# Fixed tiles for split transposes and probabilities, residual rows on DVE, other banks at the end of the FFN, and GpSimd low parts in two pieces, in a two-layer trunk on one core

## The chip, the core and the metric

One Trainium2 chip, of which the kernel uses one core. The metric is the device time of one execution in microseconds (us). Engines are named as the profile names them: PE (matrix multiplications), PEld (its weight loads), DVE (vector), ACT (scalar), POOL (GpSimd) and SP (which only issues DMAs here). Each engine works through its own list of instructions strictly in order; an instruction whose input is not ready holds up all that stand behind it on that engine.

## The reference

Two post-norm decoder layers on x of 1 x 1024 tokens x 1024 channels in float32. Layer 0 mixes with a causal pooling mixer and a Mamba-2 scan, layer 1 with two kinds of attention of eight heads each; after each mixer comes a SwiGLU network (FFN), and both have a residual and a LayerNorm.

```python
def block_causal_attention(q, k, v, log_decay_cum):      # 8 heads, 64 wide
    sc = jnp.einsum('bhqd,bhkd->bhqk', qi, k).astype(F32) * scale
    if fi is not None:                                    # FoX: forgetting gate
        sc = sc + fi[..., :, None] - log_decay_cum[:, :, None, :]
    sc = jnp.where(kpos[None, :] <= qpos[:, None], sc, -jnp.inf)
    p = jax.nn.softmax(sc, axis=-1).astype(v.dtype)
    return jnp.einsum('bhqk,bhkd->bhqd', p, v)

def odd_mixer(x, ...):                                    # layer 1
    o_fox = block_causal_attention(heads(qf), heads(kf), heads(vf), fcum)
    o_mla = block_causal_attention(q, k, kv[..., MLA_NOPE:], None)   # low-rank q and kv
    return jnp.concatenate([o_fox, o_mla], axis=-1) @ w_out

def swiglu(x, w_gate, w_up, w_down):
    return (jax.nn.silu(x @ w_gate) * (x @ w_up)) @ w_down

for l in range(2):
    h = even_mixer(x, ...) if l % 2 == 0 else odd_mixer(x, ...)
    x = layer_norm(DEEPNORM_ALPHA * x + h, ln_mix_g[l], ln_mix_b[l])
    x = layer_norm(DEEPNORM_ALPHA * x + swiglu(x, ...), ln_ffn_g[l], ln_ffn_b[l])
```

## The kernel before

**Split operands.** Every float32 operand of a product is split in two: `hi` (L196, ACT) rounds it to the matmul's own type, and `lo` (L204, or L206 with a scale; DVE, or GpSimd where the caller says so) subtracts that from the original. A product is then three matmuls: high by high, low by high, high by low (L237 to L239 for projections, L499 to L501 in the FFN, L635 to L637 in its second half, L1600 for scores, L1670 for probabilities by values, where one tile holds both parts). Weights are loaded raw (`load_raw`, L225, tile `wr`), then split into `wh` and `wl`.

**Slots.** Nearly all tiles of 128 x 1024 come from one pool, `big`, of 50 slots (`self.slot`). The tile library decides when the kernel is built, by a scheduler that walks the program in its written order and starts what is ready, in which order each engine's instructions stand and which slot a tile gets. A tile in a slot that another tile held must wait until every instruction that used the old tile has ended; that wait stands in the instruction that writes the new tile.

**Attention** (about 1090 to 1930 us of the execution). Sixteen heads come in eight pairs, four of FoX and then four of MLA. `chain` walks them in steps (head, block of 256 queries); `filler` lets the projections of the coming pairs, with their weight loads (`units_y`), run in between. A step is: scores on PE (`qk`, L1600), row maximum on DVE (L1621 or L1625), exponential on ACT (L1623 or L1626), scaling on DVE (L1631), all in a tile `prob`; then `pv` turns the probabilities by PE transposes (L1652) into a PSUM bank `p`, splits each into a tile `pt` (high part on ACT by L196, low part on DVE by L204; the triangular block goes to a tile `diag` that is kept for it), multiplies with the values (L1670) and adds the two halves of the result (`otmp` on ACT L1674, `ot` on DVE L1675). Both `prob` and `pt` take a slot of the pool for each use. PE does all this in order, so a `pt` that is late holds it.

**Residual rows.** While the attention runs, a generator `late` rescales the residual of the first layer for the second: eight times it loads 128 rows (SP queue, tile `resr`), multiplies and adds on GpSimd (L442, L443) and stores the rows by a DMA on GpSimd's queue (L444). `chain` advances it at every odd step from the second pair on (L1747).

**FFN.** Each block of the hidden layer takes seven products; each goes to a PSUM bank that `bank()` hands out from the cycle `turn` of six tags (L504): `p0` to `p3` are four banks and `pa` two more. DVE adds the products up (L527 to L542). `second()` then starts its own products (L635) in `p0` to `p3`. There are 146 calls of `bank()` in each FFN; 146 is 24 times 6 and 2 more, so the last two products (i = 4 and i = 3, added up in L542 and L540) lie in the first two banks of the cycle.

**Weight loads ahead.** `units_y` keeps `ahead + dma_ahead` raw weights loading ahead of their use (L837), `dma_ahead` being 2.

## Time and profile before

| | |
|---|---|
| time, median of 3 runs | 2545.56 us (2543.9 to 2548.15) |
| profiled execution | 2546.77 us |
| its span (first to last instruction) | 2544.7 us |
| mean granted TensorE clock | 0.986 of full speed |
| PE busy | 2449.8 us (96%) |
| DVE busy | 1824.6 us (72%) |
| ACT busy | 1044.6 us (41%) |
| POOL busy | 758.2 us (30%) |

The profiled execution lies 1.2 us above the median, and 2.07 us of it lie outside the span. PE is at work nearly all the time, so the span is what PE must do plus what it stands still, 94.9 us in all. "Busy" includes that a matmul takes longer where the clock is low: of the two levels, full speed is 2.4 GHz (1.0) and the lower is 1.2 GHz (0.5); the mean over a stretch tells how the two were mixed. In a list of waits, "A <- B" says that A stood still until B had ended.

### The profile page before, as it was taken

The numbers are of one execution on the slowest core, as the hardware profiler recorded it, in microseconds if no ns is written. First come the engines' busy times: TensorE is split into PE (matmuls) and PEld (weight loads), VectorE is DVE, ScalarE is ACT, GpSimd is POOL, SyncE is SP. The second block draws the span as 40 slices with busy tenths as digits, with TensorE's granted clock in tenths as the row PEclk, the third lists the DMA queues.
The fourth block names the chain that finished last, engine by engine and source line by source line (L and its number), as shares of the span: only waits on it lengthen the run. The fifth ranks groups of instructions, "written<-read, shape, count | busy, mean of one in ns | idle before, by whom it ended". The sixth has DMA issues, their size and how long they took to land. (4 is left out here: it accounts for less than half of the span.)

```text
span 2544.7 us, 31623 instructions
## 1 busy us (share of the span) xinstructions
PE 2449.8 (96%) x11886; PEld 2002.8 (79%) x11886; DVE 1824.6 (72%) x2907; ACT 1044.6 (41%) x1758; POOL 758.2 (30%) x446
## 2 busy tenths in 40 slices
PE   8999999999999999999998899998999999999998
PEld 6788877778888878887786777777877888887887
DVE  4365554788777779974645467787779778777988
ACT  3343344352222234454544356665544232233453
POOL 2454442113443441111113333111011433433113
PEclk9999999999999999999999899998999999999999
DMA  4111114124333347332011122012322433426641
GB/s 172 50 34 42 34 42 164 56 79 153 133 133 128 133 168 283 119 105 96 26 50 62 63 69 63 19 42 93 115 83 95 149 121 124 149 99 257 215 153 71
DMA packets 95257, 269.87 MB, mean 106 GB/s; under 512 B 9952, under 2 KB 10208, under 8 KB 95104
## 3 DMA queue, kind: packets, MB, share of 16 engines
q1 hardware_dynamic: 85632, 234.75, 26.8%
q0 software_dynamic: 6720, 23.13, 2.5%
q10 hardware_dynamic: 2752, 9.96, 1.1%
q8 instruction: 94, 1.54, 0.3%
q14 instruction: 59, 0.48, 0.1%
HBM read 190.08 MB, written 75.50 MB: 104 GB/s over the span
## 5 line engine op out<-in xcount | busy, mean ns | idle before, releaser
L204 DVE TENSOR_TENSOR w<-wr,w 128x512 fp32r<-128x512 f32 x440 | 415.7, 968 | 105.4 <-ACT w L196 99.6
L196 ACT CAST w<-wr 128x512 fp32r<-128x512 f32 x440 | 251.6, 619 | 424.2 <-DVE wr L482 331.7
L499 PE MATMUL p<-x,w 128*128 128x512 f32 x848 | 331.9, 393 | 6.4 <-ACT w L196 4.8
L500 PE MATMUL p<-x,w 128*128 128x512 f32 x848 | 331.2, 391 | 0.1
L501 PE MATMUL p<-x,w 128*128 128x512 f32 x848 | 331.2, 391 | 0.0
L547 POOL TENSOR_TENSOR h<-h,c 128x1024 f32<-128x1024 f32 x44 | 114.5, 2602 | 572.3 <-DVE c L540 420.2
L204 POOL TENSOR_TENSOR wl<-wr,wh 128x1024 fp32r<-128x1024 f32 (+2 forms) x55 | 128.2, 2333 | 358.7 <-ACT wh L196 292.0
L499 PEld LDWEIGHTS p<-x,w 128*128 128x128 f32 x848 | 159.7, 188 | 43.2 <-ACT w L196 6.3
L500 PEld LDWEIGHTS p<-x,w 128*128 128x128 f32 x848 | 159.8, 188 | 33.6 <-DVE x L204 1.2
L501 PEld LDWEIGHTS p<-x,w 128*128 128x128 f32 x848 | 159.7, 188 | 33.7 <-DVE w L204 0.8
L499 PE MATMUL pa<-x,w 128*128 128x512 f32 x384 | 149.4, 389 | 0.0
L500 PE MATMUL pa<-x,w 128*128 128x512 f32 x384 | 149.4, 389 | 0.0
L501 PE MATMUL pa<-x,w 128*128 128x512 f32 x384 | 149.4, 389 | 0.0
L239 PE MATMUL pa<-xh,wl 128*128 128x512 f32 x368 | 144.4, 392 | 4.4 <-POOL wl L204 4.4
L237 PE MATMUL pa<-xh,wh 128*128 128x512 f32 x368 | 146.7, 399 | 1.9 <-ACT u L904 1.1
L238 PE MATMUL pa<-xl,wh 128*128 128x512 f32 x368 | 144.1, 392 | 0.0
L635 PE MATMUL p<-w,h 128*128 128x512 f32 x352 | 136.9, 390 | 3.6 <-DVE c L542 3.6
L636 PE MATMUL p<-w,h 128*128 128x512 f32 x352 | 137.4, 391 | 1.9 <-DVE w L204 1.8
L637 PE MATMUL p<-w,h 128*128 128x512 f32 x352 | 136.8, 389 | 0.0
L204 DVE TENSOR_TENSOR h<-hr,h 128x512 fp32r<-128x512 f32 x154 | 123.4, 801 | 10.8 <-ACT h L196 10.7
L196 ACT CAST h<-hr 128x512 fp32r<-128x512 f32 x154 | 95.3, 619 | 73.9 <-DMA hr<-parts 37.6
L1652 PE MATMUL p<-con,prob 128*128 128x128 f32 x576 | 95.4, 283 | 8.6 <-DVE pt L204 4.9
(408 smaller groups left out, 6024.8 us busy)
## 6 DMA issues: line engine op xcount, KB each, us to landing
hr<-parts SPq DMA_DIRECT2D x70, 512.0 KB, 4.2
wr<-in_ffn_w_gate_dram SPq DMA_DIRECT2D x44, 512.0 KB, 3.8
wr<-in_ffn_w_up_dram SPq DMA_DIRECT2D x44, 512.0 KB, 4.2
wr<-in_ffn_w_down_dram SPq DMA_DIRECT2D x44, 512.0 KB, 8.8
parts<-s SPq DMA_DIRECT2D x80, 256.0 KB, 2.1
accr<-rows SPq DMA_DIRECT2D x32, 512.0 KB, 3.6
parts<-h SPq DMA_DIRECT2D x60, 256.0 KB, 2.1
wr<-in_even_wt_dram SPq DMA_DIRECT2D x24, 512.0 KB, 3.8
```

The source lines that it names most:

```text
L196: self.nc.scalar.copy(out=out, in_=in_)
L204: eng.tensor_tensor(out=out, in0=in_, in1=hi.bitcast(F32), op=ALU.subtract)
L237: mm(out=out, lhsT=lh, rhs=rh, start=i == 0, stop=False)
L238: mm(out=out, lhsT=lh, rhs=rl, start=False, stop=False)
L239: mm(out=out, lhsT=ll, rhs=rh, start=False, stop=i == n - 1)
L499: mm(out=out, lhsT=ah, rhs=b[k][:, lo], start=k == 0, stop=False)
L500: mm(out=out, lhsT=ah, rhs=b[k][:, hi], start=False, stop=False)
L501: mm(out=out, lhsT=al, rhs=b[k][:, lo], start=False, stop=k == 3)
L547: pt(out=h, in0=h, in1=c, op=ALU.mult)
L635: mm(out=out, lhsT=ah, rhs=b[:, lo], start=first, stop=False)
L636: mm(out=out, lhsT=ah, rhs=b[:, hi], start=False, stop=False)
L637: mm(out=out, lhsT=al, rhs=b[:, lo], start=False, stop=last)
```

## The change

Six edits. `lo` on GpSimd splits a tile of more than 512 columns into two operations (512 and the rest). The two operations of `late` on the residual rows go to DVE; a pause is put between them, and `chain` advances `late` at every step instead of every odd one, so that a row still takes two steps; the load stays on SP's queue, the store on GpSimd's. The cycle of FFN banks begins with `pa`, `pa`. `dma_ahead` is 1 in the odd layer. `pt` has two fixed tiles and `prob` four, which are taken from the pool once and handed out in turn.

```diff
--- before.py
+++ after.py
@@ -200,7 +200,10 @@
 
     def lo(self, out, in_, hi, scale=None, eng=None):
         eng = eng or self.nc.vector
-        if scale is None:
+        if eng is self.nc.gpsimd and scale is None and len(out.shape) == 2 and out.shape[1] > 512:
+            for s in (slice(0, 512), slice(512, out.shape[1])):
+                eng.tensor_tensor(out=out[:, s], in0=in_[:, s], in1=hi[:, s].bitcast(F32), op=ALU.subtract)
+        elif scale is None:
             eng.tensor_tensor(out=out, in0=in_, in1=hi.bitcast(F32), op=ALU.subtract)
         else:
             eng.scalar_tensor_tensor(out=out, in0=in_, scalar=scale, in1=hi.bitcast(F32),
@@ -439,8 +442,9 @@
             yield
             for t in range(NT):
                 r = self.load_raw(store[t * P:(t + 1) * P, :], name="res")
-                nc.gpsimd.tensor_tensor(out=r, in0=r, in1=v[0], op=ALU.mult)
-                nc.gpsimd.tensor_tensor(out=r, in0=r, in1=v[1], op=ALU.add)
+                nc.vector.tensor_tensor(out=r, in0=r, in1=v[0], op=ALU.mult)
+                yield
+                nc.vector.tensor_tensor(out=r, in0=r, in1=v[1], op=ALU.add)
                 nc.gpsimd.dma_start(out=store[t * P:(t + 1) * P, :], in_=r)
                 yield
 
@@ -501,7 +505,7 @@
                 mm(out=out, lhsT=al, rhs=b[k][:, lo], start=False, stop=k == 3)
 
         hid = {}
-        turn = itertools.cycle(("p0", "p1", "p2", "p3", "pa", "pa"))
+        turn = itertools.cycle(("pa", "pa", "p0", "p1", "p2", "p3"))
 
         def bank():
             tag = next(turn)
@@ -1573,6 +1577,7 @@
 
         def filler():
             self.grain = self.odd_grain
+            self.dma_ahead = 1
             misc_weight()
             self.preload(units, self.pre_n, ws)
             for g, u in zip(lead, units):
@@ -1609,10 +1614,10 @@
             prob = []
             n = [x.shape[1] for x in S]
             if sum(n) <= 1024:
-                t = self.slot(name="prob")
+                t = turn("prob")
                 prs = [t[:, :n[0]], t[:, n[0]:n[0] + n[1]]]
             else:
-                prs = [self.slot(name="prob")[:, :x] for x in n]
+                prs = [turn("prob")[:, :x] for x in n]
             l = self.small((P, 2), "l", bufs=6)
             for i, (s, pr) in enumerate(zip(S, prs)):
                 nk = n[i]
@@ -1637,6 +1642,13 @@
             for c in (0, 512):
                 nc.vector.tensor_copy(out=t[:, c:c + P], in_=self.zerob)
 
+        kept = {n: [self.slot(dt=d, name=n) for _ in range(c)] for n, d, c in (("pt", F32R, 2), ("prob", F32, 4))}
+
+        def turn(n):
+            if not kept[n]:
+                return self.slot(dt=F32R if n == "pt" else F32, name=n)
+            return kept[n][self.turn_of(n, len(kept[n]))]
+
         def pv(prob, vv, u, ot, e):
             nj = 2 * u + 2
             hl = {}
@@ -1651,7 +1663,7 @@
                         if j <= 2 * u + x:
                             nc.tensor.transpose(out=ps[:, c:c + P], in_=prob[x][:, j * P:(j + 1) * P],
                                                 identity=self.ident)
-                t = diag[self.turn_of("diag", self.n_diag)] if last else self.slot(dt=F32R, name="pt")
+                t = diag[self.turn_of("diag", self.n_diag)] if last else turn("pt")
                 b = P if last else 0
                 self.hi(t[:, b:512], ps[:, b:512])
                 self.lo(t[:, 512 + b:1024], ps[:, b:512], t[:, b:512])
@@ -1744,7 +1756,7 @@
                     products, nF, vv = pr[0][e]
                     if pend and self.tr_first[kind]:
                         next(pend[0])
-                    if n and i % 2:
+                    if n:
                         next(late, None)
                     prob, scale = softmax(qk(products, u), nF)
                     pend.append(pv(prob, vv, u, pr[1], e))
```

Counted in the kernel before, the lines from L204 on stand three lower after the change, from L443 on four, from L1576 on five and from L1645 on twelve.

How the order of instructions moves shows at three places. In these rows a name ends in a number that tells tiles apart; `PE`, `DVE`, `Activation` and `Pool` in the brackets are engines that the instruction waits for, `DMAHW` a DMA of SP's or ACT's queue, `DMASW` one of GpSimd's.

ACT at about 1345 to 1365 us of the execution, in the FoX pairs, before: exponentials (L1623), high parts of the transposes (L196 `pt`, `diag`), squares of the latent rows (L1395), and one weight.

```order
L1623 ACTIVATE prob_10440,l_10442<-prob_10440,nm_10443 128x640 [waits DVE_49]
L1623 ACTIVATE prob_10441,l_10442<-prob_10441,nm_10446 128x768 [waits DVE_49,Activation_49]
L196 CAST pt_10455<-p_1617_10450 128x512 [waits DMASW1_49,PE_49,Pool_49]
L196 CAST diag_8972<-p_1620_10473 128x384 [waits PE_49,Activation_49]
L1395 ACTIVATE sq_10365<-p_1603_10366 128x512 [waits DVE_49,PE_49,Activation_49]
L1674 COPY otmp_10493<-p_1616_10449 64x256 [waits PE_49]
L1623 ACTIVATE prob_10511,l_10513<-prob_10511,nm_10514 128x640 [waits DVE_49]
L1623 ACTIVATE prob_10512,l_10513<-prob_10512,nm_10517 128x768 [waits DVE_49]
L1395 ACTIVATE sq_10365<-p_1619_10460 128x512 [waits DVE_49]
L196 CAST pt_10532<-p_1630_10527 128x512 [waits PE_49,Pool_49]
L196 CAST wh_10540<-wr_10163 128x1024 [waits DMAHW0_49,PE_49]
L196 CAST pt_10558<-p_1638_10553 128x512 [waits Pool_49]
```

The same stretch on ACT after (L1628 is the exponential, L1686 the copy to `otmp`):

```order
L1628 ACTIVATE prob_9007,l_10455<-prob_9007,nm_10456 128x640 [waits DVE_49]
L196 CAST pt_9006<-p_1590_10463 128x512 [waits PE_49,Activation_49]
L1628 ACTIVATE prob_9008,l_10455<-prob_9008,nm_10459 128x768 [waits DVE_49]
L196 CAST diag_9002<-p_1592_10485 128x384 [waits PE_49,Activation_49]
L1686 COPY otmp_10505<-p_1589_10462 64x256 [waits PE_49,Activation_49]
L1628 ACTIVATE prob_9009,l_10525<-prob_9009,nm_10526 128x640 [waits DVE_49]
L196 CAST wh_10377<-wr_10180 128x1024 [waits DMAHW7_49,PE_49]
L1628 ACTIVATE prob_9010,l_10525<-prob_9010,nm_10529 128x768 [waits DVE_49]
L196 CAST pt_9005<-p_1600_10539 128x512 [waits PE_49]
L196 CAST pt_9006<-p_1607_10565 128x512 [waits PE_49,Activation_49]
L1628 ACTIVATE prob_9007,l_10624<-prob_9007,nm_10625 128x384 [waits DVE_49]
L196 CAST diag_9002<-p_1608_10588 128x384 [waits PE_49,Activation_49]
```

All three `pt` before wait for GpSimd, and the first also for a DMA of its queue; after, the `pt` wait for PE and for ACT's own earlier work, and they stand in the two tiles 9005 and 9006 in turn. `prob` stands in the tiles 9007 to 9010 in turn. Over the whole attention 18 of the 96 casts to `pt` wait for GpSimd before and none after.

DVE at the first residual rows, before (no row of `late` is on DVE; L1621 is the row maximum, ISA a custom operation, L1629 the reciprocal, L1631 the scaling):

```order
L204 TENSOR_TENSOR diag_8972<-p_1573_10222,diag_8972 128x384 [waits Activation_49]
L1621 ISA prob_10262,nm_10267<-pa_10255,nF_10192 128x1024 [waits PE_49]
L1621 ISA nm_10267 128x1
L1675 TENSOR_TENSOR ot_9410<-p_1572_10221,otmp_10238 64x256 [waits Activation_49]
L1394 COPY craw_10169<-p_1558_10171 128x512 [waits PE_49]
L1629 RECIPROCAL l_10263<-l_10263 128x2 [waits Activation_49]
L1631 TENSOR_SCALAR prob_10261<-prob_10261,l_10263 128x896 [waits DVE_49]
L1631 TENSOR_SCALAR prob_10262<-prob_10262,l_10263 128x1024
L204 TENSOR_TENSOR diag_8972<-p_1585_10277,diag_8972 128x384 [waits Activation_49]
L1675 TENSOR_TENSOR ot_10199<-p_1584_10276,otmp_10296 64x256 [waits Activation_49]
```

And after, with L445 and L447 the multiplication and addition of the residual rows:

```order
L207 TENSOR_TENSOR diag_9002<-p_1555_10243,diag_9002 128x384 [waits Activation_49]
L1626 ISA prob_9009,nm_10285<-pa_10275,nF_10210 128x1024 [waits PE_49]
L1626 ISA nm_10285 128x1
L1687 TENSOR_TENSOR ot_9448<-p_1554_10242,otmp_10259 64x256 [waits Activation_49]
L445 TENSOR_TENSOR resr_10266<-resr_10266,lnv_10218 128x1024 [waits DMAHW4_49,DMAHW0_49,DMAHW6_49,DMASW7_49,Pool_49]
L1634 RECIPROCAL l_10281<-l_10281 128x2 [waits Activation_49]
L447 TENSOR_TENSOR resr_10266<-resr_10266,lnv_10220 128x1024 [waits DMASW0_49,DVE_49]
L1636 TENSOR_SCALAR prob_9008<-prob_9008,l_10281 128x896 [waits DVE_49]
L207 TENSOR_TENSOR diag_9002<-p_1564_10295,diag_9002 128x384 [waits Activation_49]
L1636 TENSOR_SCALAR prob_9009<-prob_9009,l_10281 128x1024
```

The two operations of a row of 128 stand among the softmax and the low parts; L445 waits for the load (`DMAHW`), and behind it stand the reciprocal and the scaling of the step.

ACT where the last MLA weights go over to the output projection, before: loads from `spill` that ACT itself issues (L225; others come by SP) and the casts to `wh`.

```order
L196 CAST qh_13705<-qr_13704 128x1024 [waits DVE_49,Pool_49]
L196 CAST diag_8972<-p_2328_13931 128x384 [waits PE_49]
L196 CAST wh_13886<-wr_13330 128x1024 [waits DMAHW6_49]
L225 DMA wr_13890<-spill 128x1024
L196 CAST wh_13892<-wr_13698 128x1024 [waits DMAHW7_49]
L1674 COPY otmp_13945<-p_2302_13853 64x256 [waits PE_49]
L196 CAST wh_13898<-wr_13884 128x1024 [waits DMAHW1_49]
L225 DMA wr_13902<-spill 128x1024
L196 CAST wh_13904<-wr_13890 128x1024 [waits DMAHW2_49]
L196 CAST wh_13910<-wr_13896 128x1024 [waits DMAHW3_49]
L196 CAST wh_13914<-wr_13902 128x1024 [waits DMAHW4_49]
L196 CAST wh_13918<-wr_13908 128x1024 [waits DMAHW5_49]
```

And after (L228 is the load, L1631 the exponential):

```order
L196 CAST qh_13623<-qr_13622 128x1024 [waits DVE_49]
L228 DMA wr_13795<-spill 128x1024
L196 CAST wh_13797<-wr_13615 128x1024 [waits DMAHW6_49,Pool_49]
L1686 COPY otmp_13861<-p_2156_13765 64x256 [waits PE_49]
L1631 ACTIVATE prob_9009,l_13876<-pa_13867,nm_13877 128x128 [waits DVE_49]
L196 CAST pt_9006<-p_2188_13884 128x512 [waits PE_49]
L196 CAST wh_13803<-wr_13795 128x1024 [waits DMAHW0_49]
L196 CAST pt_9005<-p_2189_13897 128x512 [waits PE_49]
L228 DMA wr_13808<-spill 128x1024
L196 CAST wh_13810<-wr_13801 128x1024 [waits DMAHW1_49]
L1631 ACTIVATE prob_9009,l_13876<-pa_13867,nm_13880 128x256 [waits DVE_49]
L196 CAST pt_9006<-p_2191_13916 128x512 [waits DVE_49,PE_49]
```

Before, seven casts `wh` stand nearly together, and the tile `wr_13698` that the second of them reads was loaded 26 rows earlier; after, ACT's first load, `wr_13795`, stands five rows ahead of its cast, and casts of `pt` and exponentials stand between the casts to `wh`.

## Rows read from the trace of the kernel before

**Rows 1.** The page, busy time by engine: us, share of the span, instructions.

```profile
PE 2449.8 (96%) x11886; PEld 2002.8 (79%) x11886; DVE 1824.6 (72%) x2907; ACT 1044.6 (41%) x1758; POOL 758.2 (30%) x446
```

**Rows 2.** Windows: length, busy us of PE, PEld, DVE, ACT, POOL, clock, DMA share, GB/s.

```profile
1088.00:1920.00 832.00, 774.06 (x4187) 629.14 (x4186) 558.35 (x1095) 428.80 (x819) 172.76 (x102) 0.97 0.20 65
1344.00:1408.00 64.00, 57.04 (x269) 43.09 (x269) 35.68 (x67) 29.95 (x60) 22.36 (x11) 0.92 0.21 66
1408.00:1472.00 64.00, 57.02 (x292) 46.70 (x291) 34.21 (x66) 26.55 (x50) 18.86 (x11) 0.89 0.18 58
1472.00:1536.00 64.00, 56.39 (x283) 42.97 (x282) 43.75 (x67) 35.66 (x64) 29.71 (x19) 0.97 0.25 77
1536.00:1600.00 64.00, 60.38 (x332) 48.29 (x331) 45.46 (x97) 37.85 (x80) 15.74 (x16) 0.97 0.18 46
1728.00:1792.00 64.00, 56.64 (x311) 45.95 (x309) 46.75 (x80) 30.21 (x68) 10.65 (x4) 0.89 0.25 82
```

**Rows 3.** Waits of PE by what ended them: us in all, times, longest us.

```profile
PE p L1670 <- ACT pt L196: 12.8, 10, 3.1
...
PE p L238 <- DVE wl L204: 5.9, 4, 2.1
PE p L1652 <- DVE pt L204: 4.9, 4, 2.5
...
PE pa L239 <- POOL wl L204: 4.4, 2, 2.8
...
PE p L635 <- DVE c L542: 3.6, 2, 1.8
...
PE p L1652 <- DVE prob L1631: 3.4, 3, 1.4
...
PE p L237 <- DVE qs L206: 1.5, 1, 1.5
```

**Rows 4.** Timeline of ACT, 1326 to 1368 us: start, us, instruction, [idle before <- releaser].

```profile
1342.65 0.58 ACT L196 CAST pt<-p 128x512 fp32r<-128x512 f32 x1 [6.02 <-DMA store<-resr]
...
1365.24 0.58 ACT L196 CAST pt<-p 128x512 fp32r<-128x512 f32 x1 [2.45 <-POOL wl L204]
```

**Rows 5.** Timeline of PE, 1365 to 1372 us.

```profile
1365.88 0.58 PE L1670 MATMUL p<-pt,fv 128*128 128x256 f32 x1 [3.01 <-ACT pt L196]
...
1370.75 0.63 PE L1600 MATMUL pa<-kl,qs 128*128 128x512 f32 x1
```

**Rows 6.** The page, costliest groups: busy us, mean ns of one, idle before.

```profile
L500 PE MATMUL p<-x,w 128*128 128x512 f32 x848 | 331.2, 391 | 0.1
```

**Rows 7.** Timeline of DVE, 1366 to 1378 us.

```profile
1371.19 2.33 DVE L1631 TENSOR_SCALAR prob<-prob,l 128x384 f32<-128x384 f32 x1
...
1375.60 0.48 DVE L1631 TENSOR_SCALAR prob<-prob,l 128x512 f32<-128x512 f32 x1
```

**Rows 8.** Timeline of POOL, 1320 to 1380 us.

```profile
1370.95 2.36 POOL L442 TENSOR_TENSOR resr<-resr,lnv 128x1024 f32<-128x1024 f32 x1 [5.75 <-DMA resr<-store]
```

**Rows 9.** Timeline of DVE, 1470 to 1482 us.

```profile
1472.35 4.31 DVE L1631 TENSOR_SCALAR prob<-prob,l 128x384 f32<-128x384 f32 x2
```

**Rows 10.** Groups of POOL by form: busy us, mean ns, idle before and releaser.

```profile
L204 POOL TENSOR_TENSOR wl<-wr,wh 128x1024 fp32r<-128x1024 f32 x47 | 115.7, 2464 | 338.6 <-ACT wh L196 271.9 <-PE p L1670 18.9 <-PE pa L239 18.4
...
L442 POOL TENSOR_TENSOR resr<-resr,lnv 128x1024 f32<-128x1024 f32 x8 | 19.7, 2460 | 57.1 <-DMA resr<-store 57.1
...
L204 POOL TENSOR_TENSOR wl<-wr,wh 128x512 fp32r<-128x512 f32 x4 | 5.1, 1280 | 4.1 <-ACT wh L196 4.0
```

**Rows 11.** Groups of DVE by form.

```profile
L204 DVE TENSOR_TENSOR wl<-wr,wh 128x1024 fp32r<-128x1024 f32 x16 | 25.6, 1613 | 8.4 <-ACT wh L196 8.3
...
L1162 DVE TENSOR_TENSOR cv<-cv,z 128x1024 f32<-128x1024 f32 x8 | 9.8, 1226 | 17.9 <-POOL cv L1160 17.9
```

**Rows 12.** DMA issues: transfer, queue, count, KB each, median us from issue to landing.

```profile
resr<-store SPq DMA_DIRECT2D x8, 512.0 KB, 3.7
```

**Rows 13.** Timeline of ACT, 1724 to 1746 us.

```profile
1734.43 3.89 ACT L196 CAST wh<-wr 128x1024 fp32r<-128x1024 f32 x4 [3.59 <-DMA wr<-spill]
```

## The prediction

> **What bounds the kernel now.** I read the busy times first: PE works 2449.8 of 2544.7 us [rows 1], so an edit changes the time only where PE stands still, or where its clock is low. The windows come next, to find where that is. Of the 95 us in which PE stands, 58 lie in the attention: from 1088 to 1920 us it works 774.06 of 832, and the mean granted clock is 0.97 there [rows 2]. The windows of 64 us that show it most are those from 1344 to 1536, where PE stands about 7 us in each, at a clock of 0.92, 0.89 and 0.97, and the one from 1728, with 7.4 us and 0.89. Third the list of what PE waited for [rows 3]: the largest entry is the product of probabilities by values (L1670), which waited 12.8 us in ten pieces for ACT's high part `pt`. Then the timelines of ACT and DVE at those places, to see what ACT and DVE in turn waited for.
>
> ACT had not waited for the transposes there. The cast to `pt` at 1342.65 stood 6.02 us until a store of residual rows was through, the one at 1365.24 stood 2.45 us until GpSimd had ended a weight's low part [rows 4]. Neither is an input of the cast: both had been working on the slot that the new `pt` got. PE's wait of 3.01 us ends with the second of them [rows 5]. Five microseconds later a matmul of 512 columns takes 0.63 us [rows 5] instead of 0.39 [rows 6]: the chip has put PE on the lower of its two levels, after a row of such stops.
>
> **Part 1, fixed `pt` and `prob`.** A fixed `pt` was last read by L1670 two tiles earlier, and on PE those matmuls stand ahead of the transposes that the next cast waits for anyway, so that reuse adds no wait of its own. The 18 casts that waited for GpSimd wait for PE and ACT alone. Of the 12.8 us I take 10, because some waits for ACT remain where ACT is simply late. Ends: 0 (the wait comes back elsewhere) and 12.8.
>
> With these stops goes some of the low clock. A mean of 0.92 over 64 us is 64 x 0.08 = 5.1 us of full-speed work lost, and likewise 7.0 in 1408 to 1472, 1.9 in each of the next two windows and 7.0 in the one from 1728, together 22.9 [rows 2]. I credit the windows in which I find `pt` stops ahead of the drop, 5.1 + 1.9 + 1.9 = 9. Ends: 0 and 22.9.
>
> **Part 2, the residual rows on DVE, and GpSimd's operations in halves.** At 1371.19 a scaling of 384 columns took 2.33 us, while one of 512 columns at 1375.60 took 0.48 [rows 7]; GpSimd's L442 had begun at 1370.95 and taken 2.36, so that DVE was let through when it ended [rows 8]. At 1472.35 two scalings took 4.31 together, one behind L442, the other behind its twin L443 [rows 9]. Such holds reach PE as its waits for DVE's `pt` (4.9 us, longest 2.5), `qs` (1.5) and `prob` (3.4 in three) [rows 3]. With L442 and L443 gone from GpSimd I credit 2.5 + 1.5 = 4. The weights' low parts stay, in pieces of 1.280 us instead of 2.464 [rows 10], a hold shorter by 1.18; for two of the `prob` waits I credit 1 each, 2 together. That makes 6. Ends: 0, because the two halves can hold two DVE operations one after the other as in [rows 9], and 4.9 + 3.4 + 1.5 = 9.8.
>
> The halves also let PE begin on the first 512 columns of a weight. It waited twice for such a weight, 4.4 us [rows 3]; 1.18 each makes 2.4. Ends 0 and 2.4. GpSimd pays 2 x 1.280 - 2.464 = 0.1 us for each of some 60 tiles, 6 us, while it is idle 70% of the span [rows 1]; free.
>
> Against it DVE gets 16 operations of 1024 columns with both inputs in SBUF. The nearest row is L1162, 1.226 us [rows 11]: 19.6 us. They fall at 1330 to 1530 us, where DVE is busy 34 to 44 of 64 us [rows 2]. With somewhat over half of DVE's time taken, most of them find a gap, and I put a quarter on PE's path: 5 us. Ends: 0 and 19.6. DVE's low parts of weights, also of 1024 columns and two SBUF inputs, took 1.613 on the mean [rows 11], 0.39 above L1162, in stretches where GpSimd works on weights too. The Trainium skill (SBUF — State Buffer, section "SBUF: two separate sides") says that a DVE operation with two SBUF inputs contends with a GpSimd operation that reads SBUF, and that the second to start waits for the whole of the other. The 1.613 agrees with that. By the rule the moved operations could themselves be held up to 1.28 each, 16 x 1.28 = 20.5 more on DVE, and a quarter of that would add 5 us to the sum; by the row's mean excess it would be 16 x 0.39 / 4 = 1.6, and I leave it in the rounding of the quarter.
>
> A wait is added, too. L445 waits for the load of its rows, and DVE is in order: behind it stand the reciprocal and the scaling of the step, then low parts, and PE's transposes wait for these. The load takes 3.7 us from issue to landing [rows 12], and its issue waits in SP's queue for a slot. GpSimd waited 57.1 us for the eight loads [rows 10], at no cost, having nothing urgent behind. For DVE I take 1 us each, half of it reaching PE: 4 us. Ends: 0 (the load is early, since a pause lies between the steps) and 8 x 3.7 = 29.6, where DVE arrives as the load is issued.
>
> **Part 3, the FFN's banks.** The second half's first product (L635) waited twice, 1.8 us each, for L542 to read its bank [rows 3]. The last two products now lie in the two `pa` banks and the first products of the second half use `p0` to `p3`, read earlier. Credit 3.6, ends 0 and 3.6. Nothing is late next: the weights and `h` that it also needs are split on DVE ahead of L542.
>
> **Part 4, the handover and the slots.** At 1734.43 four casts of weights began 3.59 us late, behind a load from `spill` [rows 13]; PE's 5.9 us of waiting for DVE's `wl` [rows 3] are the same place. After, the first load that ACT issues stands only five rows ahead of its cast instead of 26. I charge 4 us, one such wait more. Ends: a gain of 5.9 (the casts now stand apart, and others pass between) and a loss of 7.2, two waits. With one weight less loaded ahead and six tiles held for good, the waits for a slot that `pt` had fall to the casts `wh`, which wait for GpSimd or its DMAs more often now. They feed projections that run ahead of their use; 3 us, with the ends 0 and 12.8.
>
> **The sum.** Credits 10 + 9 + 6 + 2.4 + 3.6 = 31, debits 5 + 4 + 4 + 3 = 16: 15 us less. The profiled execution took 2546.8 us (span 2544.7 and 2.1 around it), so 2531.8; as it lies 1.2 above the median of the runs, I predict 2531.
>
> **Rivals.** (1) The waits only change their place: a cast `wh` that waits for a slot stands in ACT's list ahead of `pt` and exponentials, and holds them as `pt` itself did. For it: all 50 slots are still handed from one owner to the next, and six fewer go round. Against it: a `wh` is needed later than a `pt`. Then the 10 and the 9 are lost and the 3 is not paid on top: -12 + 13 = +1, about 2547.
>
> (2) Slower: DVE stands at L445. If SP issues the loads only as DVE arrives, DVE stands 3.7 us at each of eight, 29.6 in place of 4, and PE's stops keep the clock low, 9 back: -15 + 25.6 + 9 = +20, 2565. For it: the 57.1 us that GpSimd waited, and that the loads wait for slots in SP's queue. Against it: DVE reaches L445 behind a full step of softmax. It decides from (15 + 4) / 8 = 2.4 us that reach PE at each row, without any drop of the clock.
>
> (3) More is gained: with fewer stops the clock stays up in all five windows. Credits 12.8 + 22.9 + 9.8 + 2.4 + 3.6 = 51.5, less 16: 2510 against the median. Against it: the stops at the handover and those for `diag` have other causes.
>
> **Chances.** The forecast 0.55, with its own range of 2520 to 2541; rival 1 0.18, rival 2 0.15, rival 3 0.12. A measurement of this kernel tells about 0.2%, 5.1 us, from no change, so faster means below 2540.5 and slower above 2550.7. Faster is 0.52 of the forecast, 0.04 of rival 1 and all 0.12 of rival 3: 0.68. Same is 0.03, 0.11 and 0.02 of rival 2: 0.16. Slower is 0.03 and 0.13: 0.16. The range of 2509 to 2553 takes in rivals 3 and 1, and leaves out most of rival 2 and a little below.
>
> **What would show it.** Right: no cast to `pt` that ends a wait for GpSimd or a store, PE's wait for ACT `pt` below 3 us, the clock at 0.97 or more from 1344 to 1408, no scaling above 1.5 us, L635 without its 1.8 us. Wrong: idle time of DVE ahead of L445 ended by the load, several microseconds at a time, with PE's waits for `prob` or `pt` behind it; casts `wh` with several microseconds of idle time ahead, ended by GpSimd or a store; a longer stop of PE at the handover.

## The result and the profile after

| | before | after |
|---|---|---|
| time, median | 2545.53 us (2543.9 to 2548.15, 4 runs) | 2512.14 us (2506.4 to 2514.39, 4 runs) |
| ratio after to before | | 0.9864, 95% interval 0.9844 to 0.9884 |
| span of the profiled execution | 2544.7 us | 2512.3 us |
| PE busy | 2449.8 us | 2441.0 us |
| PE standing (span less busy) | 94.9 us | 71.3 us |
| mean granted clock | 0.986 | 0.989 |

The kernel became 33 us faster by the medians, 34.6 by the ratio, where 15 had been forecast; the time lies in the range, near its lower end, and 2 us above the value of the third rival. The span fell by 32.4 us: PE stands 23.6 us less, and its own work takes 8.8 us less because the clock is low for less time.

The first view is the page's busy times after, which answer to [rows 1].

```profile
PE 2441.0 (97%) x11886; PEld 2002.4 (80%) x11886; DVE 1819.6 (72%) x2923; ACT 1046.8 (42%) x1758; POOL 732.7 (29%) x493
```

DVE is busy 5 us less than before although it has 16 operations more. The windows after answer to [rows 2] (length, busy us of PE, PEld, DVE, ACT and POOL, clock, DMA share, GB/s); the attention now ends some 30 us sooner, so that the first window is 800 us long, the handover to the output projection lies in the one from 1696, and the last one is the end of the first FFN.

```profile
1088.00:1888.00 800.00, 765.03 (x4195) 625.20 (x4194) 555.88 (x1115) 431.85 (x823) 141.12 (x121) 0.98 0.21 68
1344.00:1408.00 64.00, 58.17 (x285) 45.41 (x284) 41.23 (x80) 31.41 (x64) 14.85 (x12) 0.95 0.24 83
1408.00:1472.00 64.00, 60.81 (x325) 49.59 (x324) 43.24 (x75) 30.49 (x55) 14.41 (x11) 0.95 0.22 75
1472.00:1536.00 64.00, 60.23 (x312) 47.48 (x312) 46.73 (x93) 40.32 (x79) 19.52 (x24) 0.97 0.26 71
1536.00:1600.00 64.00, 60.64 (x342) 48.79 (x341) 46.67 (x88) 40.79 (x82) 14.38 (x13) 1.00 0.15 41
1696.00:1760.00 64.00, 59.67 (x339) 48.53 (x338) 46.83 (x84) 34.48 (x73) 11.06 (x8) 0.97 0.34 116
936.00:1088.00 152.00, 148.99 (x646) 122.74 (x645) 140.67 (x202) 62.15 (x111) 33.24 (x25) 0.98 0.53 185
```

In the attention PE stands 35 us instead of 58, 5.8 of them from 1344 to 1408 (7.0 before). From 1408 to 1536 it stands 3 to 4 us in each window instead of 7, at 0.95 and 0.97; the handover window stands at 4.3 us and 0.97 instead of 7.4 and 0.89. What PE waited for, after (us in all, times, longest), answers to [rows 3]:

```profile
PE p L503 <- ACT w L196: 6.9, 2, 3.5
...
PE p L640 <- DVE w L207: 6.0, 2, 3.0
PE p L1682 <- DVE diag L207: 5.8, 4, 2.8
PE p L1682 <- ACT diag L196: 3.8, 5, 1.2
PE p L1682 <- ACT pt L196: 3.0, 5, 1.1
PE p L1664 <- DVE prob L1636: 2.5, 3, 0.9
...
PE pa L242 <- POOL wl L205: 2.2, 2, 1.7
...
PE p L1664 <- DVE pt L207: 1.1, 3, 0.5
...
PE p L241 <- DVE wl L207: 1.0, 3, 0.5
```

ACT's `pt` went from 12.8 to 3.0 us, DVE's `pt` from 4.9 to 1.1, DVE's `wl` from 5.9 to 1.0, GpSimd's `wl` from 4.4 to 2.2. Two entries are new or longer: L640 for a low part of `w` (6.0 us, 1.8 before) and `diag` from DVE (5.8, 2.0 before). The group of the casts to `pt` shows what went with the `pt` wait, before and then after (busy us, mean ns, idle time before them and what ended it):

```profile
L196 ACT CAST pt<-p 128x512 fp32r<-128x512 f32 x96 | 55.6, 586 | 70.0 <-PE p L1652 43.7 <-POOL wl L204 9.9 <-DMA store<-resr 6.0
```

```profile
L196 ACT CAST pt<-p 128x512 fp32r<-128x512 f32 x96 | 55.6, 585 | 45.7 <-PE p L1664 43.5 <-DVE l L1634 1.3
```

The idle time ended by GpSimd and by the store of residual rows, 15.9 us, is gone, and none for a slot has taken its place. The residual rows on DVE, as groups by form, with the weights' low parts on DVE, which answer to [rows 11]:

```profile
L207 DVE TENSOR_TENSOR wl<-wr,wh 128x1024 fp32r<-128x1024 f32 x16 | 20.5, 1288 | 6.4 <-ACT wh L196 6.1 <-PE pa L1605 0.2
...
L445 DVE TENSOR_TENSOR resr<-resr,lnv 128x1024 f32<-128x1024 f32 x8 | 13.6, 1698 | 7.3 <-DMA resr<-store 7.2
...
L447 DVE TENSOR_TENSOR resr<-resr,lnv 128x1024 f32<-128x1024 f32 x8 | 10.3, 1282 | 0.1
```

L445 takes 1.698 us on the mean and not 1.226, since three of the eight are held by a GpSimd operation. DVE stood 7.2 us ahead of it, in two pieces. Behind the first, of 2.42 us, PE waits: L445 stands ahead of the low part of a `diag`, and PE stood 2.55 us until that was done, which is nearly half of its 5.8 us for `diag`. Behind the second, of 4.82 us, PE does not stand. The rows of DVE and then of PE at the first piece:

```profile
1350.15 1.23 DVE L445 TENSOR_TENSOR resr<-resr,lnv 128x1024 f32<-128x1024 f32 x1 [2.42 <-DMA resr<-store]
1351.30 0.55 DVE L207 TENSOR_TENSOR diag<-p,diag 128x384 fp32r<-128x384 f32 x1
```

```profile
1351.90 0.62 PE L1682 MATMUL p<-diag,fv 128*128 128x256 f32 x3 [2.55 <-DVE diag L207]
```

The `wl` came down from 1.613 to 1.288 us.

### The profile page after: what moved, and what is told of

The parts are those of the page before. It is cut to its first block, busy times and chain, and to the rows that moved or that the text cites. A ratio compares the mean times of both kernels' runs of the same rounds, so it can differ in the third digit from the quotient of the medians.

```text
span 2512.3 us, 31696 instructions
## 1 busy us (share of the span) xinstructions
PE 2441.0 (97%) x11886; PEld 2002.4 (80%) x11886; DVE 1819.6 (72%) x2923; ACT 1046.8 (42%) x1758; POOL 732.7 (29%) x493
## 3 DMA queue, kind: packets, MB, share of 16 engines
q1 hardware_dynamic: 85632, 234.75, 27.2%
## 5 line engine op out<-in xcount | busy, mean ns | idle before, releaser
L196 ACT CAST w<-wr 128x512 fp32r<-128x512 f32 x440 | 251.6, 619 | 432.1 <-DVE wr L486 337.9
L503 PE MATMUL p<-x,w 128*128 128x512 f32 x832 | 325.6, 393 | 6.9 <-ACT w L196 6.9
L505 PE MATMUL p<-x,w 128*128 128x512 f32 x832 | 324.9, 391 | 0.0
L504 PE MATMUL p<-x,w 128*128 128x512 f32 x832 | 324.8, 390 | 0.0
L205 POOL TENSOR_TENSOR wl<-wr,wh 128x512 fp32r<-128x512 f32 x102 | 136.1, 1355 | 354.5 <-ACT wh L196 261.0
L503 PEld LDWEIGHTS p<-x,w 128*128 128x128 f32 x832 | 157.1, 189 | 39.9 <-ACT w L196 7.8
L505 PEld LDWEIGHTS p<-x,w 128*128 128x128 f32 x832 | 156.8, 188 | 33.1 <-DVE w L207 0.6
L504 PEld LDWEIGHTS p<-x,w 128*128 128x128 f32 x832 | 157.0, 189 | 32.2
L503 PE MATMUL pa<-x,w 128*128 128x512 f32 x400 | 155.8, 389 | 0.0
L504 PE MATMUL pa<-x,w 128*128 128x512 f32 x400 | 155.6, 389 | 0.0
L505 PE MATMUL pa<-x,w 128*128 128x512 f32 x400 | 155.6, 389 | 0.0
L242 PE MATMUL pa<-xh,wl 128*128 128x512 f32 x368 | 144.5, 393 | 2.2 <-POOL wl L205 2.2
L640 PE MATMUL p<-w,h 128*128 128x512 f32 x352 | 139.1, 396 | 6.0 <-DVE w L207 6.0
L196 ACT CAST h<-hr 128x512 fp32r<-128x512 f32 x154 | 95.2, 618 | 77.6 <-DMA hr<-parts 37.8
L641 PE MATMUL pa<-w,h 128*128 128x512 f32 x264 | 102.8, 389 | 0.0
```

The source lines that it names most:

```text
L196: self.nc.scalar.copy(out=out, in_=in_)
L205: eng.tensor_tensor(out=out[:, s], in0=in_[:, s], in1=hi[:, s].bitcast(F32), op=ALU.subtract)
L242: mm(out=out, lhsT=ll, rhs=rh, start=False, stop=i == n - 1)
L503: mm(out=out, lhsT=ah, rhs=b[k][:, lo], start=k == 0, stop=False)
L504: mm(out=out, lhsT=ah, rhs=b[k][:, hi], start=False, stop=False)
L505: mm(out=out, lhsT=al, rhs=b[k][:, lo], start=False, stop=k == 3)
```

## The experiments

All ratios are to the kernel before, run beside it on the same chip; a gain in us is one less the ratio, times 2545.5. An interval of 0.0015 to each side is 4 us. Where two of the runs are compared with each other, or one with the kernel after, both intervals count, together some 5 to 7 us. The runs are numbered in the order in which they were made; each quoted text says first which kernel it is.

**Edits alone.** First the fixed tiles, with the shorter load-ahead that they need.

```diff
+            self.dma_ahead = 1
+        kept = {n: [self.slot(dt=d, name=n) for _ in range(c)] for n, d, c in (("pt", F32R, 2), ("prob", F32, 4))}
...
-                t = diag[self.turn_of("diag", self.n_diag)] if last else self.slot(dt=F32R, name="pt")
+                t = diag[self.turn_of("diag", self.n_diag)] if last else turn("pt")
```

> 

> The kernel before with the fixed tiles for pt and prob and dma_ahead 1, nothing else of the change (the fixed tiles need the shorter load-ahead, since six slots fewer go round). Theory A (the credits of the prediction for part 1 hold, 10 of waiting and some 9 of clock, and the charge for waits that move to the weights is nothing): 19 to 22 us less than before, about 2525, PE's wait for ACT pt at 3 us or less. Theory B (the waits only move to the casts of weights and hold ACT there): within 5 us of before, the pt waits gone but idle time of ACT ahead of wh up by 8 us or more. Theory C (the gain of the whole change is mainly the residual rows' leaving GpSimd): below 8 us less here.

Measured (first run) 2523.81 us, ratio 0.9909 (0.9895 to 0.9923): 23.2 us. That is theory A's size, with PE's wait for ACT's `pt` at 4.1 us and not 3 or less; theories B and C are out.

Next the residual rows alone:

```diff
-                nc.gpsimd.tensor_tensor(out=r, in0=r, in1=v[0], op=ALU.mult)
-                nc.gpsimd.tensor_tensor(out=r, in0=r, in1=v[1], op=ALU.add)
+                nc.vector.tensor_tensor(out=r, in0=r, in1=v[0], op=ALU.mult)
+                yield
+                nc.vector.tensor_tensor(out=r, in0=r, in1=v[1], op=ALU.add)
...
-                    if n and i % 2:
+                    if n:
```

> 

> The kernel before with only the residual rows on DVE and their new pace. The prediction's sum for this part (4 credited, 5 and 4 charged): about 5 us more, 2550, with DVE's idle time ahead of the multiplication ended by the load near 8 us. Theory C (the holds of DVE behind GpSimd cost more than was credited, and the added DVE work falls into gaps): 8 to 15 us less, 2531 to 2538, scaling operations of 384 columns back below 0.5 us on the mean. Theory A: within 5 us of before.

Measured (second run) 2528.16 us, 0.9926 (0.9912 to 0.9939): 18.8 us faster, where the prediction's own sum said 5 slower and theory C 8 to 15 faster. DVE's idle time ahead of the multiplication, ended by the load, is 2.1 us. The scalings of 384 columns came down from 793 to 587 ns on the mean, not below the 0.5 us of theory C. This was the clearest miss.

The halves alone:

```diff
+        if eng is self.nc.gpsimd and scale is None and len(out.shape) == 2 and out.shape[1] > 512:
+            for s in (slice(0, 512), slice(512, out.shape[1])):
```

> 

> The kernel before with only GpSimd's low parts in two operations. The prediction: 2.4 for PE's earlier start on a weight and 2 for shorter holds of DVE, 4 us less, about 2541, PE's wait of L239 for POOL wl from 4.4 to about 2. A rival, that halves hold two DVE operations one after the other: 2 us less, 2543. A larger gain of 10 or more would say that holds behind the weights' low parts, not those behind the residual rows, were the cost.

Measured (third run) 2541.55 us, 0.9979 (0.9968 to 0.9989): 5.3 us, and L242's wait for `wl` is 2.2 us. The size is as forecast. Of the shorter holds of DVE, for which 2 us had been credited, the waits show no gain: PE's wait for `prob` is 2.6 us instead of 3.4, that for DVE's `pt` 5.7 instead of 4.9.

One weight less ahead, alone:

```diff
+            self.dma_ahead = 1
```

> 

> The kernel before with only dma_ahead 1 in the odd layer. If loading ahead is not what limits: within 3 us of before, 2546; this run then shows, too, how much a mere change of the order of instructions moves the time. If a slot more for the others is what helps: 5 to 10 us less, with fewer pt casts that end a wait for GpSimd. If weights come late: 5 to 10 more, with PE waiting for wh or wl.

Measured (fourth run) 2534.20 us, 0.9952 (0.9939 to 0.9965): 12.2 us. So about half of the first run's gain needs no fixed tile.

**What the rows' gain is made of.** Two GpSimd operations whose results nobody is shown waiting for, after each row (in the trace the row's store is issued between the two, so about 2.4 us later than without them):

```diff
                 nc.vector.tensor_tensor(out=r, in0=r, in1=v[1], op=ALU.add)
+                nc.gpsimd.tensor_tensor(out=v[1], in0=v[1], in1=v[0], op=ALU.add)
+                nc.gpsimd.tensor_tensor(out=v[1], in0=v[1], in1=v[0], op=ALU.subtract)
```

> 

> The kernel of the second run (only the residual rows on DVE), and after each row two operations of 128 x 1024 on GpSimd that read two tiles of SBUF, add one LayerNorm vector to the other and take it away again, so that GpSimd has as much to do as before and nobody waits for it. ACT's, DVE's and PE's order stay nearly the same. If the gain of 17.7 us came from DVE no longer being held behind L442 and L443: 8 to 15 us slower than the second run, 2536 to 2543, with scaling operations of 2 us and more again. If it came from the row's slot and store coming free sooner, or from GpSimd's queue: within 4 us of it, 2525 to 2532, though DVE is held as often.

Measured (fifth run) 2554.68 us, 1.0021 (1.0011 to 1.0031): 24 us slower than the second run, more than the 8 to 15 expected. Two rows of DVE's timeline and the GpSimd rows beside them show the holds (start, us, instruction, idle time before):

```profile
1317.31 5.68 DVE L1634 TENSOR_SCALAR prob<-prob,l 128x896 f32<-128x896 f32 x2
...
1341.67 3.20 DVE L1634 TENSOR_SCALAR prob<-prob,l 128x640 f32<-128x640 f32 x2
```

```profile
1317.06 2.38 POOL L445 TENSOR_TENSOR lnv<-lnv,lnv 128x1024 f32<-128x1024 f32 x1 [11.68 <-DVE l L1632]
...
1320.06 2.37 POOL L446 TENSOR_TENSOR lnv<-lnv,lnv 128x1024 f32<-128x1024 f32 x1
...
1341.90 2.56 POOL L445 TENSOR_TENSOR lnv<-lnv,lnv 128x1024 f32<-128x1024 f32 x1 [8.37 <-DVE resr L444]
```

Two scalings of 896 and more columns, 1.5 us together when undisturbed, took 5.68 from 1317.31 on, and ended at 1322.99, just after the second GpSimd operation (1322.43). From 1341.67 on the first of two ran and the second waited until 1344.46. PE's waits for DVE, in the second run and then in this one:

```profile
PE p L1653 <- DVE prob L1632: 3.4, 3, 1.4
...
PE p L1653 <- DVE pt L204: 2.0, 3, 1.2
...
PE p L1671 <- DVE diag L204: 2.0, 3, 0.7
```

```profile
PE p L1655 <- DVE pt L204: 8.9, 8, 3.1
...
PE p L1655 <- DVE prob L1634: 8.2, 6, 2.2
PE p L1673 <- DVE diag L204: 7.8, 3, 6.5
```

They rise from 7.4 to 24.9 us in these groups, with ACT's and DVE's work in nearly the same order (about a dozen rows of each stand elsewhere). In the profiles PE stands 99.8 us instead of 82.4, and its own work takes 2456.4 instead of 2444.1, at the lower clock. The rise of these waits is as large as the rise of PE's standing: what this run loses is for the most part the holds.

It does not follow that the second run gained by losing holds. Its operations don't stand just where L442 and L443 stood, and the same three groups made 10.3 us in the kernel before (4.9, 3.4 and 2.0), not 24.9. Of the 12.5 us that PE stands less in the second run, 7.4 are waits for ACT: for `pt` 9.1 instead of 12.8 us [rows 3], for `diag` 0.5 instead of 4.2. Two lines of before that [rows 3] leaves out, and then the second run's:

```profile
PE p L1670 <- ACT diag L196: 4.2, 2, 3.7
...
PE p L1670 <- DVE diag L204: 2.0, 3, 0.7
```

```profile
PE p L1671 <- ACT pt L196: 9.1, 8, 3.1
...
PE p L1671 <- ACT diag L196: 0.5, 1, 0.5
```

They do not come back in the fifth run (8.8 and 0.7). The cast to `pt` that waited 6.0 us for the store of a row is gone in the second run, and stays away in the fifth:

```profile
L196 ACT CAST pt<-p 128x512 fp32r<-128x512 f32 x96 | 55.7, 587 | 59.3 <-PE p L1653 38.2 <-POOL wl L204 10.1 <-PE p L238 6.0
```

So a part of the rows' gain hangs on the rows' own move. The missing wait points at the slot of the row, but no run separates this from the order.

The pace alone, with both operations left on GpSimd:

```diff
                 nc.gpsimd.tensor_tensor(out=r, in0=r, in1=v[0], op=ALU.mult)
+                yield
                 nc.gpsimd.tensor_tensor(out=r, in0=r, in1=v[1], op=ALU.add)
...
-                    if n and i % 2:
+                    if n:
```

> 

> The kernel before with the new pace of late (a pause between the two operations, advanced at every step), both operations still on GpSimd. If the engine matters and the pace doesn't: within 5 us of before, 2541 to 2551. If the pace alone brings the gain of the second run, by another order: 2530 to 2536, with the wait of 3 us at 1343 and of 3.7 at 1442 gone.

Measured (sixth run) 2546.55 us, 0.9992 (0.9980 to 1.0004): nothing. The engine matters.

**Edits taken out of the whole.** The rows back on GpSimd in the kernel after:

```diff
-                nc.vector.tensor_tensor(out=r, in0=r, in1=v[0], op=ALU.mult)
-                yield
-                nc.vector.tensor_tensor(out=r, in0=r, in1=v[1], op=ALU.add)
+                nc.gpsimd.tensor_tensor(out=r, in0=r, in1=v[0], op=ALU.mult)
+                nc.gpsimd.tensor_tensor(out=r, in0=r, in1=v[1], op=ALU.add)
...
-                    if n:
+                    if n and i % 2:
```

> 

> The kernel after with the residual rows back on GpSimd at the old pace. If the gains add up: 17.7 us slower than after, 2530. If fixed tiles and rows had removed the same waits of pt for a slot in part, so that they overlap (22 + 17.7 + 4.3 is 44 against a whole of 33): 5 to 11 us slower, 2517 to 2523. By the prediction's charges (5 and 4 for the rows on DVE against a credit of 4): 5 us faster, 2507.

Measured (seventh run) 2511.77 us, 0.9857 (0.9839 to 0.9876): 1.8 us less than after by the ratio, and both intervals together are 7. That the gains add up is out, and 5 to 11 us slower is only just out; the 5 us faster of the prediction's charges can't be excluded. PE stands 4.5 us more than in after (75.8), its work takes 6.8 less (2434.2), at a clock of 0.993. Its waits in this run, against those of after above:

```profile
PE p L1681 <- ACT pt L196: 5.7, 4, 3.8
PE p L1681 <- ACT diag L196: 5.7, 5, 3.2
PE p L1663 <- DVE pt L207: 4.1, 5, 1.5
PE p L1663 <- DVE prob L1635: 4.1, 5, 1.3
...
PE p L1681 <- DVE diag L207: 0.9, 3, 0.5
```

With the rows on DVE, as in after, the first four are 9.2 us shorter and the last is 4.9 us longer.

The FFN's banks back:

```diff
-        turn = itertools.cycle(("pa", "pa", "p0", "p1", "p2", "p3"))
+        turn = itertools.cycle(("p0", "p1", "p2", "p3", "pa", "pa"))
```

> 

> The kernel after with the FFN's banks in the old order. By the traces the wait of 1.8 us for L542 has turned into one of 3.0 for a low part of w (L640) and a longer one for L503's weight: 1 to 4 us faster than after, 2508 to 2511, the waits of L635 and L636 as in the kernel before. By the prediction (a gain of 3.6): 3.6 slower, 2516.

Measured (eighth run) 2515.45 us, 0.9865 (0.9845 to 0.9884): not told from after, so neither expectation is confirmed. Later the banks were tried alone, where the interval is narrower (the same diff, the other way round):

> 

> The kernel before with only the FFN's banks in the new order. By the prediction: 3.6 us faster, 2542. By the traces of after and of the eighth run (the wait of L635, 3.6 us, is gone, but those of L640 and L503 are 4.2 and 2.1 longer, and the clock is 0.98 instead of 1.00 from 936 to 1088): the same to 4 us slower, 2545 to 2550.

Measured (seventeenth run) 2548.94 us, 1.0008 (0.9998 to 1.0019): no gain; 3.6 us is out.

**Is it the slot?** The fourth run with 49 slots:

```diff
-        self.big = ctx.enter_context(tc.tile_pool(name="big", bufs=50))
+        self.big = ctx.enter_context(tc.tile_pool(name="big", bufs=49))
```

> 

> The fourth run (the kernel before with dma_ahead 1) with 49 slots in the pool instead of 50. If the 11 to 12 us of the fourth run came from the slot that one weight less leaves to the others: most of it is gone, 2540 to 2546, with more waits of casts to pt and wh for GpSimd. If they came from another order alone, or from fewer loads: 2531 to 2536, as in the fourth run.

Measured (ninth run) 2552.46 us, 1.0028 (1.0019 to 1.0037): the whole gain is gone and 7.1 us more. The casts to `pt`, in the fourth run and in this one:

```profile
L196 ACT CAST pt<-p 128x512 fp32r<-128x512 f32 x96 | 55.5, 586 | 63.2 <-PE p L1653 44.9 <-PE p L239 7.4 <-POOL wl L204 4.3
```

```profile
L196 ACT CAST pt<-p 128x512 fp32r<-128x512 f32 x96 | 55.5, 587 | 71.4 <-PE p L1653 45.8 <-POOL wl L204 9.9 <-DMA store<-resr 6.0
```

With the slot taken away the waits for GpSimd's `wl` (9.9 us) and the store (6.0) stand there as in the kernel before, to a tenth. ACT's idle time ahead of the casts to `wh` goes the same way: 25.9 us before, 9.7 in the fourth run, 29.2 in this one. The slot is worth 19 us here. Two things stay open. The others have as many slots in this run as before, and the 7.1 us are not explained by their number; and the order of the instructions changes with the pool, so that slot and order are told apart only by the waits that name a slot's last user.

The halves taken out of the kernel after:

```diff
-            for s in (slice(0, 512), slice(512, out.shape[1])):
-                eng.tensor_tensor(out=out[:, s], in0=in_[:, s], in1=hi[:, s].bitcast(F32), op=ALU.subtract)
```

> 

> The kernel after with GpSimd's low parts whole again. If the halves are worth what they were worth alone (4 us): 2516. If they are worth more once pt no longer waits for slots (the rows and the banks were worth nothing on top of the rest, so that 10 to 13 of the 33 us are left for the halves): 2521 to 2525. Holds: scaling operations of more than 1.5 us again, the sum of the scaling up by 5 us or more.

Measured (tenth run) 2510.76 us, 0.9865 (0.9848 to 0.9882): no difference to after within the intervals, which leave room for the 4 us of the halves alone but not for 10. All scalings together take 2 us more and not 5.

The fixed tiles taken out of it, for `prob` likewise:

```diff
-                t = diag[self.turn_of("diag", self.n_diag)] if last else turn("pt")
+                t = diag[self.turn_of("diag", self.n_diag)] if last else self.slot(dt=F32R, name="pt")
```

> 

> The kernel after with pt and prob from the pool again, all else of the change kept (dma_ahead 1, rows on DVE, halves, banks). If the fixed tiles add what they added to dma_ahead alone (10 us): 2522. If rows, halves and one weight less have taken the same waits away already: 2511 to 2515, with casts to pt that wait for GpSimd still there but short.

Measured (eleventh run) 2515.93 us, 0.9878 (0.9861 to 0.9895): 3.6 us by the ratio, within both intervals; 10 us would lie at their edge. PE's wait for ACT's `pt` is 3.3 us, against 3.0 with the fixed tiles.

Rows and banks taken out of it, so that tiles, load-ahead and halves are left:

```diff
-                nc.vector.tensor_tensor(out=r, in0=r, in1=v[0], op=ALU.mult)
+                nc.gpsimd.tensor_tensor(out=r, in0=r, in1=v[0], op=ALU.mult)
...
-        turn = itertools.cycle(("pa", "pa", "p0", "p1", "p2", "p3"))
+        turn = itertools.cycle(("p0", "p1", "p2", "p3", "pa", "pa"))
```

> 

> Fixed tiles, dma_ahead 1 and the halves; rows on GpSimd and banks as before. If rows and banks bring nothing on top: 2509 to 2514, like the kernel after. If either is worth something only where the other is left out: 2518 or more.

Measured (twelfth run) 2514.77 us, 0.9876 (0.9860 to 0.9893): 3.1 us from after by the ratio, again within the intervals.

**How far the edits overlap.** Load-ahead and rows, on the kernel before:

```diff
+            self.dma_ahead = 1
...
-                nc.gpsimd.tensor_tensor(out=r, in0=r, in1=v[0], op=ALU.mult)
+                nc.vector.tensor_tensor(out=r, in0=r, in1=v[0], op=ALU.mult)
```

> 

> The kernel before with dma_ahead 1 and the residual rows on DVE; no fixed tiles, no halves, banks as before. If the edits take mostly different waits away: 12 + 18 = 30 us less than before, 2516. If a slot more and the rows' leaving are the same waits: 18 to 22 less, 2524 to 2528.

Measured (thirteenth run) 2519.23 us, 0.9893 (0.9877 to 0.9908): 27.2 us of 12.2 + 18.8 = 31.0. These two are mostly different waits.

The kernel after with the needless GpSimd operations of the fifth run:

```diff
+                nc.gpsimd.tensor_tensor(out=v[1], in0=v[1], in1=v[0], op=ALU.add)
+                nc.gpsimd.tensor_tensor(out=v[1], in0=v[1], in1=v[0], op=ALU.subtract)
```

> 

> The kernel after with the two needless GpSimd operations per residual row of the fifth run (24 us there). If holds behind GpSimd cost PE only where slots are short: 0 to 6 us slower than after, 2512 to 2518, though DVE's scaling is held as often. If they cost the same everywhere: 15 to 24 us slower, 2527 to 2536.

Measured (fourteenth run) 2528.86 us, 0.9933 (0.9915 to 0.9951): 17.6 us slower than after. Holds cost PE nearly as much where slots are no longer short; the first expectation is out. One row of DVE's timeline, two scalings of 896 and more columns, while GpSimd ran the first needless operation, a weight's low part and the second needless one (1474.91 to 1482.71):

```profile
1475.56 7.72 DVE L1638 TENSOR_SCALAR prob<-prob,l 128x896 f32<-128x896 f32 x2
```

No extra weight loaded ahead, on the kernel after and on the one before:

```diff
-            self.dma_ahead = 1
+            self.dma_ahead = 0
```

> 

> The kernel after with dma_ahead 0. If slots are still short: 3 to 8 us faster, 2504 to 2509. If they are no longer short, or weights now come late: the same to 8 slower, 2512 to 2520, with PE waiting for wh or wl in the attention.

Measured (fifteenth run) 2515.31 us, 0.9882 (0.9864 to 0.9899): 4.6 us more by the ratio, and the intervals overlap; the 3 to 8 us faster is out.

> 

> The kernel before with dma_ahead 0. If the second slot helps as the first did (12 us): 2522 to 2530. If the first took what there was: 2530 to 2537. If weights now come late: slower than the fourth run, above 2537.

Measured (sixteenth run) 2532.50 us, 0.9947 (0.9933 to 0.9960): 13.5 us, as with 1. A second weight less brings nothing more that can be measured.

None of the versions is shown to be faster than the kernel after; those with tiles, rows, halves or banks taken out can't be told from it.

## Why the prediction was wrong

The credits came to 31 us, and the traces show 32.4 less. Of this 23.6 is standing, against 10 + 6 + 2.4 + 3.6 = 22 credited, and 8.8 is the clock, against 9. The 16 us of charges didn't come as a loss of time. But that the totals meet is in part chance, and each step has to be taken by itself. The clock shows it: as far as the windows before and after can be compared, the three that were credited with 9 us gave back 3.8 (0.92 to 0.95, 0.97 to 0.97, 0.97 to 1.00). The rest came from two that were not credited, 1408 to 1472 (0.89 to 0.95, 3.8 us) and the handover (0.89 to 0.97, 5.1), less some 3 us lost at the end of the first FFN. Of the signs of being right the clock from 1344 to 1408 failed (0.95, not 0.97), two scalings still took over 1.5 us (1.67 and 1.73, against eight of up to 2.80 before), and PE's wait for ACT's `pt` is at the limit of 3.

- **Fixed tiles: right in size, not shown to be theirs.** PE's wait for ACT `pt` fell by 9.8 us (10 credited), and no cast to `pt` waits for GpSimd's `wl` or a store. But without the tiles it falls nearly as far, to 3.3 and 3.1 us (eleventh and thirteenth runs): the prediction gave one edit a wait that others also take away.
- **The slots in part 4: the step that failed first.** I charged 3 us for "one weight less loaded ahead and six tiles held for good", and let the range of that term end at 0, as if loading less ahead could only cost. Measured alone, `dma_ahead` 1 gains 12.2 us, and with 49 slots it loses 7.1: by the waits that went and came back, the raw weight that was loaded early had held a slot that `pt` and `wh` were waiting for. The waits of [rows 4] were waits for a slot; I read them as a matter of who gets which slot, and not of how many there are. Tiles and load-ahead together were put at 10 + 9 - 4 - 3 = 12 and are 23.2 (first run).
- **The handover: the wrong sign.** 4 us were charged for later loads. The wait for a load ahead of a cast is 0.96 us at the longest (it was 3.59, [rows 13]), and PE's wait for DVE's `wl` fell from 5.9 to 1.0. In the first run, which has the fixed tiles, it is 1.8 already; in the second and the fourth, without them, 5.9 and 7.0. With the tiles the casts to `wh` no longer stand in one block, which may be a cause; no run changes it alone, and the halves do much of the same without the tiles (3.0 us in the third run, 2.7 in the eleventh).
- **The rows: credited too little, charged too much.** 4 us were credited, for PE's waits behind holds of DVE, against charges of 5 and 4. Alone, the rows gain 18.8 us, and of the 12.5 us that PE then stands less, 7.4 are waits for ACT's `pt` and `diag` that the prediction did not connect with the rows. In the whole, the seventh run's waits and those of after show 9.2 us taken away and 4.9 added. The mechanism of the hold was right, and holds can cost much more than 4 us: the fifth run lost 24, in the profiled executions 17.4 of standing and 12.3 of PE's own work at a lower clock. But these were holds of that run's own making. What the rows are worth in the whole is not told from nothing: 1.8 us the other way, within 7.
- **The wait for the rows' loads: there, and smaller than charged.** 7.2 us of DVE's idle time in two pieces; 8 were assumed, and 4 for PE. What reaches PE is 2.55 us, at 1351.90, behind the first piece and the L445 that follows it. This was one of the signs of being wrong, with `diag` in the place of `prob` or `pt`.
- **Halves: right in size**, 4.4 forecast and 5.3 measured alone; L239's wait went from 4.4 to 2.2, the 2.4 credited for it. The 2 for shorter holds is not borne out by the third run's waits; PE's wait for DVE's `wl` fell there instead, from 5.9 to 3.0. On top of the rest they are worth nothing that can be measured.
- **Banks: wrong.** L635 no longer waits, but PE then stands a few products later, for a low part of `w` that is split on DVE:

```profile
950.81 0.79 PE L640 MATMUL p<-w,h 128*128 128x512 f32 x1 [3.01 <-DVE w L207]
```

That is 3.01 us instead of 0.9, in each FFN, L503 waits 6.9 instead of 4.8, and the clock from 936 to 1088 is 0.98. I had written that nothing is late next, since `w` and `h` are split ahead of L542: that holds for the first product, not for the second weight.

The rivals: (1) is out, for ACT's casts to `wh` wait less (20.0 us before them instead of 25.9). The group before and then after:

```profile
L196 ACT CAST wh<-wr 128x1024 fp32r<-128x1024 f32 (+1 forms) x71 | 70.9, 1010 | 25.9 <-PE p L238 9.4 <-DMA store<-resr 5.2 <-DMA wr<-spill 3.6
```

```profile
L196 ACT CAST wh<-wr 128x1024 fp32r<-128x1024 f32 (+1 forms) x71 | 71.4, 1010 | 20.0 <-PE p L1415 5.7 <-issue 3.6 <-POOL ql L205 3.3
```

(2) is out: DVE stood 7.2 and not 29.6 us. (3) named the time, but not the way: the clock kept drops in the windows from 1344 to 1536, and `diag` waits grew.

**The overlap.** Alone, the edits gain 12.2 (load-ahead), 23.2 - 12.2 = 11.0 (tiles on top of it), 18.8, 5.3 and -2.0: 45.3 us; together 34.6. Load-ahead and tiles bring 23.2, and then either the halves (31.6, twelfth run) or the rows with the new banks (34.4, tenth run) bring nearly all the rest. Load-ahead, tiles and rows take the same wait away, PE's for ACT's `pt`, 12.8 us before. It is 9.1 in the second run (rows); here it is in the first (load-ahead and tiles), the fourth (load-ahead) and the thirteenth (load-ahead and rows):

```profile
PE p L1678 <- ACT pt L196: 4.1, 2, 3.7
```

```profile
PE p L1671 <- ACT pt L196: 6.9, 5, 2.3
```

```profile
PE p L1672 <- ACT pt L196: 3.1, 3, 1.7
```

Whichever of them comes last finds little of it left. Why halves and rows overlap too is not shown. It is not that DVE has nothing left to gain: without the 19.6 us of the rows' own work, its busy time falls from the first run's 1816.6 us by 8.0 with the halves (twelfth run), by 9.6 with the rows and banks (tenth run) and by 16.6 with both (after), so that on DVE they add up. What is left open is the clock, too. The seventh run stands longer than after and is as fast, its clock being 0.993; PE's own work takes 2441.0 us in the profiled execution of after and 2430.6 in that of the tenth run. The four executions of after alone go from 2506.4 us at 0.992 to 2514.39 at 0.987. Which stops pull the clock down is not settled by these runs.

## What to carry to other kernels

When an instruction waits for a buffer and not for its input, the first question is how many buffers are held by work that is early; loading one tile less ahead can be worth as much as an elaborate edit (12.2 us here). Taking one buffer away is a quick test, to be read by the waits that come back, since the order of instructions changes with it. An operation moved between two engines that block each other must be priced with the holds of both, on everything that stands behind them, and with the buffer that it frees earlier or later, not with its own duration and the one wait that the list names. Edits that remove the same waiting don't add up, so that each must be timed alone and taken out of the whole before it is credited. "Nobody waits for it" must be read off the instructions behind a stop, not off the name of the stop: PE's wait for a load showed here as one for `diag`.
